# Feed-forward end of a hybrid decoder layer: the last two outputs made in two shares of tokens

## The chip, the cores and the metric

The kernel runs on one core of a Trainium2 chip. The metric is the device time of one execution in microseconds (us). Before the change three runs took 1458.08, 1457.53 and 1454.21 us; their median is 1457.53.

## The reference, cut to what matters

One decoder layer with two head groups, then a gated feed-forward network and a last RMS norm, on 320 tokens (256 of a prompt and 8 x 8 of samples) of width 2048. The part that the change touches is the end:

```python
h2 = rms_norm(x, norm_ffn)
gate, up = jnp.split(h2 @ w_ffn_in, 2, axis=-1)
x = x + (jax.nn.silu(gate) * up) @ w_ffn_out
...
y_prompt = rms_norm(xp, norm_final)
y_sample = rms_norm(xs, norm_final)
```

The hidden width is 5632. The norm of a token needs the squares of all its 2048 features, so no output can be normed before the last feature block of that token is there.

## The kernel before

Activations lie transposed: features on the 128 partitions, in `KT` = 16 blocks, and the `N` = 320 tokens along the free axis. `x1[:, n]` is block `n` of the residual, 128 x 320 in f32. Every large product is made by `gemm`: each f32 weight block is split into a rounded part `hi` (type fp32r) and a rest `lo`, the activations likewise, and three matmuls of 128x128 weights and 320 columns are added up in PSUM (lines 141 to 143). `wload` fetches the weights, up to eight 128x128 blocks at a time: SyncE issues the load (line 129), ScalarE rounds (`hi`, line 130), VectorE subtracts (`lo`, line 131). Its buffers come from a pool named by `wpool`; from the first feed-forward chunk on that is `wp2` with four raw and three split buffers, while the earlier pool `wp` also serves the sample states of the retention heads (`states_load`, `states_add`).

The hidden features are worked through in `FCH` = 4 chunks of 11 blocks. `ffn_in(c)` makes a chunk, `ffn_out(c, a)` multiplies it into the 16 outputs: for each output `n` 33 matmuls into `ps_fo`, which VectorE adds to `x1[:, n]` (lines 174 to 177, the helper `tt`; it stands in the trace as line 176). In the last chunk ScalarE also squares the finished block (`sqx`), VectorE sums the squares in `acc3`, and ScalarE multiplies the block with the norm's weight (line 1168).

The end of the program works so. `rstd_bcast` finds the norm's factor: matmuls of the squares with a column of ones give each token's sum (`ps_r`, and `ps_l` for the last block, whose square comes latest), with tokens as partitions, in three groups of 128 that begin at the tokens of `STARTS`; VectorE makes the reciprocal root in three Newton rounds (`rsqrt`, on `ms`, `ry`, `rt` of three columns); matmuls with the identity lay it out again along the tokens on all partitions (`ps_r2`, in the trace also `ps_r<-ident,ry`). In between `keep_warm` lets TensorE multiply ones. Then ScalarE copies the factor into `acc3`, VectorE scales blocks 0 to 10 from PSUM and GpSimd blocks 11 to 15 from that copy, and SyncE stores them in eight transfers, block groups by the table `TAIL`:

```python
    next(tail["rg"])
    rps = next(tail["rg"])
    act.copy(acc3, rps)
    for a_, b_ in TAIL:
        for n in range(a_, b_):
            tt(x1[:, n], x1[:, n], rps, MUL)
            if n < 5:
                pool.tensor_tensor(x1[:, 11 + n], x1[:, 11 + n], acc3, MUL)
        sp.dma_start(yT[:, a_:b_], x1[:, a_:b_])
    sp.dma_start(yT[:, 11:14], x1[:, 11:14])
    sp.dma_start(yT[:, 14:16], x1[:, 14:16])
```

TensorE and GpSimd work in the order in which the program is written; on the other engines a scheduler orders the instructions, and `tc.high_priority(offset=...)` moves those inside it ahead in that order. Every engine works through its queue in order.

Of the kernel before, what the change touches and what calls it, by code (L numbers as in the profile page):

```python
# [12 lines left out]
F32 = mybir.dt.float32  # L13
F32R = mybir.dt.float32r
I32 = mybir.dt.int32
AF = mybir.ActivationFunctionType
ALU = mybir.AluOpType
ADD, SUB, MUL = ALU.add, ALU.subtract, ALU.mult
PSUM = bass.MemoryType.PSUM

P = 128
D = 2048
KT = D // P
NP, NB, NS = 256, 8, 8
N = NP + NB * NS
# [3 lines left out]
FCH = 4  # L29
FCT = FT // FCH  # L30
# [5 lines left out]
TAIL = ((0, 1), (1, 2), (2, 3), (3, 5), (5, 8), (8, 11))  # L36
# [8 lines left out]
def hybrid_kernel(ctx, tc, xT, w_in, w_in4, w_out, w_glu, w_fi, w_fo, vecs, s5p, bc, x0,  # L45
# [3 lines left out]
    pe, act, dve, pool, sp = nc.tensor, nc.scalar, nc.vector, nc.gpsimd, nc.sync  # L49

    cst = ctx.enter_context(tc.tile_pool(name="cst", bufs=1))
    wp = ctx.enter_context(tc.tile_pool(name="wp", bufs=1))
    ps_acc = ctx.enter_context(tc.tile_pool(name="ps_acc", bufs=2, space=PSUM))

    def f(t):
        return t.bitcast(F32)
# [18 lines left out]
    def v(nm, i):  # L75
        return vec[:, voff[nm] + i:voff[nm] + i + 1]


    class Clk:
        now = 0.0  # L80
        n = 0
# [9 lines left out]
    def run_due(flush=False):  # L91
        while clk.heap and (flush or clk.heap[0][0] <= clk.now):
            t, _, gen = heapq.heappop(clk.heap)
            clk.now = max(clk.now, t)
            try:
                d = next(gen)
            except StopIteration:
                continue
            spawn(gen, d)

    def mm(cost, *a, **k):
        pe.matmul(*a, **k)
        clk.now += cost
# [8 lines left out]
    def keep_warm(n):  # L112

        pt = ps_acc.tile([P, 512], F32, name="warm_ps", tag="acc", bufs=2)
        for _ in range(n):
            pe.matmul(pt, onesr, onesr.unsqueeze(1).to_broadcast([P, 4, P]), start=True, stop=True)


    wpool = [wp, (3, 3, 3)]

    def wload(src, nk, offset=3000):

        out = []
        with tc.high_priority(offset=offset):
            for k0 in range(0, nk, 8):
                m = min(8, nk - k0)
                raw, hi, lo = (wpool[0].tile([P, 8, P], d, name=n, tag=n, bufs=wpool[1][i])
                               for i, (n, d) in enumerate((("raw", F32), ("hi", F32R), ("lo", F32R))))
                sp.dma_start(raw[:, :m], src[:, k0:k0 + m])
                act.copy(hi[:, :m], raw[:, :m])  # L130
                dve.tensor_tensor(lo[:, :m], raw[:, :m], f(hi[:, :m]), SUB)  # L131
                out += [(hi[:, i], lo[:, i]) for i in range(m)]
        return out

    def gemm(name, src, nk, xhi, xlo, ps=None, ws=None):
        ws = ws or wload(src, nk)
        if ps is None:
            pt = ps_acc.tile([P, 512], F32, name=name, tag="acc", bufs=2)
            ps = pt[:, :N]
        for k, (hi, lo) in enumerate(ws):  # L140
            pe.matmul(ps, hi, xhi[:, k], start=k == 0, stop=False)  # L141
            pe.matmul(ps, hi, xlo[:, k], start=False, stop=False)  # L142
            pe.matmul(ps, lo, xhi[:, k], start=False, stop=k == nk - 1)  # L143
            clk.now += 0.4
            if k < nk - 1:
                run_due()
        return ps
# [20 lines left out]
    def ts(out, a, s1, o1, s2=None, o2=None):  # L168
        if o2 is None:
            dve.tensor_scalar(out, a, s1, None, o1)  # L170
        else:
            dve.tensor_scalar(out, a, s1, s2, o1, o2)
        return out

    def tt(out, a, b, op):
        dve.tensor_tensor(out, a, b, op)  # L176
        return out

    def stt(out, a, s, b, o1, o2):
        dve.scalar_tensor_tensor(out, a, s, b, o1, o2)  # L180
        return out

    def rsqrt(t, y, tmp):

        ts(y.bitcast(I32), t.bitcast(I32), -0.5, MUL, float(0x1EF759DF), ADD)
        for _ in range(3):
            tt(tmp, y, y, MUL)
            tt(tmp, tmp, t, MUL)
            stt(y, tmp, 1.5, y, ADD, MUL)

    STARTS = (0, 128, 192)
# [1 line left out]
    EVAC = 1500  # L193
    GN = 1000

    def rstd_bcast(pool_, acc, ps_of, tag, last=None, dl=5.0, ytok=None):

        def sums(a, name):
            ps = ps_of(name)
            for i, s in enumerate(STARTS):  # L200
                mm(0.1, ps[:, i:i + 1], a[:, s:s + P], ones[:, 0:1], start=True, stop=True)
            return ps[:, 0:3]

        ms = pool_.tile([P, 3], F32, name="ms", tag=tag + "ms")
        y = pool_.tile([P, 3], F32, name="ry", tag=tag + "ry")
        if ytok is not None:
            ytok.append(y)
        tmp = pool_.tile([P, 3], F32, name="rt", tag=tag + "rt")
        ps = sums(acc, "ps_r")
        if last is not None:  # L210
            keep_warm(3)
        with tc.high_priority(offset=2000):
            ts(ms, ps, -0.5 / D, MUL, -0.5 * EPS, ADD)
            if last is not None:
                stt(ms, sums(last(), "ps_l"), -0.5 / D, ms, MUL, ADD)
            if last is not None:
                keep_warm(9)
            rsqrt(ms, y, tmp)
        yield dl
        ps2 = ps_of("ps_r2")  # L220
        for i, s in enumerate(STARTS):
            mm(0.22, ps2[:, s:s + P], y[:, i:i + 1].to_broadcast([P, P]), ident, start=True,
               stop=True)
        yield ps2[:, :N]
# [680 lines left out]
    with tc.issue_after(los[4].ins):  # L905
        s5_params(exps[0])
    ytok = []
    rg = rstd_bcast(s5, accq, misc, "n1", ytok=ytok)

    def finish_norm():  # L910
# [47 lines left out]
    x1 = xp.tile([P, KT, N], F32, name="x1")  # L958
# [69 lines left out]
    for n in range(KT):  # L1028
        if n == 0:
            late = gemm_late("ps_o", lambda n: w_out[n, :, 8:16], 0, 4, 8, rhi, rlo)  # L1030
        ps = late[n] if n < 2 else gemm("ps_o", w_out[n, :, 8:16], 8, rhi, rlo)
# [4 lines left out]
    for n in range(8):  # L1036
        ps = gemm("ps_g", w_glu[n], 8, yhi, ylo)
# [5 lines left out]
    hp = ctx.enter_context(tc.tile_pool(name="hp", bufs=1, reuse_waits="tile"))  # L1043
# [5 lines left out]
    def square(n, pl):  # L1049
        s = pl.tile([P, N], F32, name="sqx", tag="sqx", bufs=2)  # L1050
        act.activation(s, x1[:, n], AF.Square)
        return s

    for n in range(KT):
        if n == 0:
            late = gemm_late("ps_o2", lambda n: w_out[n, :, 0:8], 0, 6, 8, zhi, zlo)
        ps = late[n] if n < 2 else gemm("ps_o2", w_out[n, :, 0:8], 8, zhi, zlo)
# [5 lines left out]
        else:  # L1063
            s = square(n, hp)
# [7 lines left out]
    fp = ctx.enter_context(tc.tile_pool(name="fp", bufs=1, side="right", reuse_waits="tile"))  # L1072
# [5 lines left out]
    def ffn_norm():  # L1078
        rg = rstd_bcast(hp, acc2, norm_ps, "n2")
        next(rg)  # L1080
        yield DL["n2b"]
        act.copy(rbc2, next(rg))
# [65 lines left out]

    wp2 = ctx.enter_context(tc.tile_pool(name="wp2", bufs=1, reuse_waits="tile"))
    acc3 = fp.tile([P, N], F32, name="acc3")  # L1150
    tail = {}

    def ffn_out(c, a):
        for n in range(KT):
            ps = gemm("ps_fo", w_fo[c, n], FCT, *a)
            if c == FCH - 1 and n == KT - 1:
                tail["rg"] = rstd_bcast(fp, acc3, norm_ps, "n3", lambda: tail["s"])
            tt(x1[:, n], x1[:, n], ps, ADD)
            if c == FCH - 1:
                if n == 0:  # L1160
                    act.activation(acc3, x1[:, n], AF.Square)
                else:
                    s = square(n, hp)
                    if n == KT - 1:
                        tail["s"] = s
                    else:
                        tt(acc3, acc3, s, ADD)
                act.mul(x1[:, n], x1[:, n], v("g_fin", n))

    a0 = ffn_in(0)  # L1170
    a1 = ffn_in(1)
    ffn_out(0, a0)
    a2_ = ffn_in(2)
    ffn_out(1, a1)
    a3 = ffn_in(3)
    ffn_out(2, a2_)
    ffn_out(3, a3)
    next(tail["rg"])
    rps = next(tail["rg"])
    act.copy(acc3, rps)  # L1180
    for a_, b_ in TAIL:
        for n in range(a_, b_):
            tt(x1[:, n], x1[:, n], rps, MUL)
            if n < 5:
                pool.tensor_tensor(x1[:, 11 + n], x1[:, 11 + n], acc3, MUL)
        sp.dma_start(yT[:, a_:b_], x1[:, a_:b_])
    sp.dma_start(yT[:, 11:14], x1[:, 11:14])
    sp.dma_start(yT[:, 14:16], x1[:, 14:16])


def _host(inp):
# [92 lines left out]
```

## Time and profile before

| | us |
|---|---|
| median of three runs | 1457.53 |
| the profiled execution, its own time | 1454.4 |
| its span, first to last instruction | 1452.3 |
| TensorE busy in it | 1435.0 |
| VectorE busy | 852.8 |
| ScalarE busy | 607.5 |
| GpSimd busy | 80.7 |

PE is TensorE's matmuls and PEld its weight loads, DVE is VectorE, ACT ScalarE, POOL GpSimd, SP SyncE (SPq its queue, from which transfers are issued). A row gives a start or a sum in us, a length, and for a group the mean of one instruction in ns. Matmuls overlap: the length of one runs from its start to the end of its results, and a matmul can start long before the one ahead has ended, so the pace of a run is read from the distance of starts. An f32 matmul stands in the trace as two passes, each with its own weight load; an fp32r matmul as one. Times in the tables of stages and in the timelines count from the start of the span.

### The profile page before, as it was taken

How to read it: one execution, taken by the hardware profiler on the slowest of the kernel's cores; microseconds unless marked ns; L12 is line 12 of the kernel's file. 1: busy time of each engine (PE TensorE's matmuls, PEld its weight loads, DVE VectorE, ACT ScalarE, POOL GpSimd, SP SyncE). 2: the span in 40 equal slices, each digit the busy share in tenths (PEclk: the TensorE clock that was granted, in tenths of full speed). 3: DMA queues.
4: the chain of work that ended last, by engine and by line, in shares of the span. 5: the costliest groups of instructions: out<-in, count | busy, mean ns of one | idle time of the engine just before them, and what ended most of it. 6: DMA issues, size and time to landing. Idle time of an engine off the chain costs nothing.

```text
span 1452.3 us, 26302 instructions
## 1 busy us (share of the span) xinstructions
PE 1435.0 (99%) x10654; PEld 1419.5 (98%) x10654; DVE 852.8 (59%) x1402; ACT 607.5 (42%) x973; POOL 80.7 (6%) x163
## 2 busy tenths in 40 slices
PE   9999999999999999999999999999999999999997
PEld 8999999999999999999999999999999999999996
DVE  8978787777566747564444444444444444444454
ACT  7555555555355433333333333333333333333452
POOL 8520001100000000000000000000000000000001
PEclk9999999999999999999999999999999999999998
DMA  8455554555644575665444455444355444444443
GB/s 286 161 162 156 164 165 150 155 162 151 208 149 154 177 229 182 225 198 166 149 155 146 122 154 175 147 156 148 120 154 164 159 153 151 136 137 145 154 146 111
DMA packets 84712, 235.38 MB, mean 162 GB/s; under 512 B 16368, under 2 KB 32368, under 8 KB 84592
## 3 DMA queue, kind: packets, MB, share of 16 engines
q1 hardware_dynamic: 83680, 231.58, 49.8%
q10 hardware_dynamic: 912, 2.14, 0.5%
q8 instruction: 84, 1.38, 0.4%
q14 instruction: 36, 0.29, 0.1%
HBM read 222.63 MB, written 8.95 MB: 159 GB/s over the span
## 4 chain that ended last, share of the span: by engine, by line
PE 70%; DVE 1%; ACT 0%; issue 0%; DVEq 0%
PE ps_fo L142 7%; PE ps_fu L141 7%; PE ps_fo L141 7%; PE ps_fu L142 7%; PE ps_fu L143 7%; PE ps_fo L143 7%; PE ps_fg L141 7%; PE ps_fg L142 7%; PE ps_fg L143 7%; PE ps_o L141 1%; PE ps_o L142 1%; PE ps_o L143 1%; PE ps_g L142 1%; PE ps_g L143 1%; PE ps_g L141 1%; DVE x L176 0%
## 5 line engine op out<-in xcount | busy, mean ns | idle before, releaser
L131 DVE TENSOR_TENSOR lo<-raw,hi 128x1024 fp32r<-128x1024 f32 (+1 forms) x416 | 466.6, 1122 | 381.8 <-ACT hi L130 381.1
L130 ACT CAST hi<-raw 128x1024 fp32r<-128x1024 f32 (+1 forms) x416 | 402.1, 967 | 673.4 <-PE ps_fo L142 189.2
L141 PE MATMUL ps_fg<-hhi,hi 128*128 128x320 f32 x704 | 217.5, 309 | 0.0
L142 PE MATMUL ps_fo<-alo,hi 128*128 128x320 f32 x704 | 217.5, 309 | 0.0
L143 PE MATMUL ps_fo<-ahi,lo 128*128 128x320 f32 x704 | 217.5, 309 | 0.0
L141 PE MATMUL ps_fo<-ahi,hi 128*128 128x320 f32 x704 | 217.5, 309 | 0.0
L142 PE MATMUL ps_fg<-hlo,hi 128*128 128x320 f32 x704 | 217.4, 309 | 0.0
L142 PE MATMUL ps_fu<-hlo,hi 128*128 128x320 f32 x704 | 217.4, 309 | 0.0
L141 PE MATMUL ps_fu<-hhi,hi 128*128 128x320 f32 x704 | 217.4, 309 | 0.0
L143 PE MATMUL ps_fg<-hhi,lo 128*128 128x320 f32 x704 | 217.4, 309 | 0.0
L143 PE MATMUL ps_fu<-hhi,lo 128*128 128x320 f32 x704 | 217.4, 309 | 0.0
L141 PE MATMUL ps_p<-xhi,hi 128*128 128x320 f32 x560 | 177.7, 317 | 1.9 <-DVE q__1095 L176 1.4
L143 PE MATMUL ps_p<-xhi,lo 128*128 128x320 f32 x560 | 173.2, 309 | 0.0
L142 PE MATMUL ps_p<-xlo,hi 128*128 128x320 f32 x560 | 172.9, 309 | 0.0
L142 PEld LDWEIGHTS ps_fg<-hlo,hi 128*128 128x128 f32 x704 | 132.3, 188 | 0.3
L141 PEld LDWEIGHTS ps_fg<-hhi,hi 128*128 128x128 f32 x704 | 132.3, 188 | 0.3
L142 PEld LDWEIGHTS ps_fu<-hlo,hi 128*128 128x128 f32 x704 | 132.4, 188 | 0.0
L141 PEld LDWEIGHTS ps_fu<-hhi,hi 128*128 128x128 f32 x704 | 132.4, 188 | 0.0
L143 PEld LDWEIGHTS ps_fu<-hhi,lo 128*128 128x128 f32 x704 | 132.4, 188 | 0.0
L143 PEld LDWEIGHTS ps_fg<-hhi,lo 128*128 128x128 f32 x704 | 132.3, 188 | 0.0
L141 PEld LDWEIGHTS ps_fo<-ahi,hi 128*128 128x128 f32 x704 | 132.1, 188 | 0.0
L142 PEld LDWEIGHTS ps_fo<-alo,hi 128*128 128x128 f32 x704 | 132.1, 188 | 0.0
(420 smaller groups left out, 1939.4 us busy)
## 6 DMA issues: line engine op xcount, KB each, us to landing
raw<-w_fi SPq DMA_DIRECT2D x176, 512.0 KB, 3.7
raw<-w_in SPq DMA_DIRECT2D x79, 512.0 KB, 4.1
raw<-w_fo SPq DMA_DIRECT2D x64, 512.0 KB, 3.5
raw<-w_out SPq DMA_DIRECT2D x32, 512.0 KB, 3.7
raw<-w_fo SPq DMA_DIRECT2D x64, 192.0 KB, 2.4
rt<-r SPq DMA_DIRECT2D x8, 512.0 KB, 5.2
raw<-w_glu SPq DMA_DIRECT2D x8, 512.0 KB, 3.6
raw<-r SPq DMA_DIRECT2D x8, 512.0 KB, 4.3
```

What stands on the lines that cost most here:

```text
L130: act.copy(hi[:, :m], raw[:, :m])
L131: dve.tensor_tensor(lo[:, :m], raw[:, :m], f(hi[:, :m]), SUB)
L141: pe.matmul(ps, hi, xhi[:, k], start=k == 0, stop=False)
L142: pe.matmul(ps, hi, xlo[:, k], start=False, stop=False)
L143: pe.matmul(ps, lo, xhi[:, k], start=False, stop=k == nk - 1)
```

## The change

The last two outputs (`n` = 14 and 15) of the last chunk leave `ffn_out`'s loop and go to `out_tail`. It loads both weights, the second from the pool `wp`, and then goes over two shares of the tokens, 0 to 191 and 192 to 319: in each share it makes output 14 and then output 15, with matmuls of 192 and of 128 columns. The first share's squares are summed by `rstd_bcast` with two groups of tokens; its first step is written behind output 14 of the second share, its second step (the broadcast) behind output 15. `finish` scales and stores one share: it is what stood at the program's end, on a slice of the tokens. The second share has a factor of its own, one group of tokens, with the warming matmuls. `add_out` is what `ffn_out` did to an output in the last chunk.

```diff
@@ rstd_bcast @@
-    def rstd_bcast(pool_, acc, ps_of, tag, last=None, dl=5.0, ytok=None):
+    def rstd_bcast(pool_, acc, ps_of, tag, last=None, dl=5.0, ytok=None, starts=STARTS):
+        nst = len(starts)
...
-            for i, s in enumerate(STARTS):
+            for i, s in enumerate(starts):
...
@@ the end of the feed-forward part @@
+    ps_t = ctx.enter_context(tc.tile_pool(name="ps_t", bufs=2, space=PSUM))
...
     def ffn_out(c, a):
+        lastc = c == FCH - 1
+        for n in range(KT - 2 if lastc else KT):
             ps = gemm("ps_fo", w_fo[c, n], FCT, *a)
...
+        if lastc:
+            out_tail(c, a)
+
+    def finish(rps, sl):
+        acc = acc3[:, sl]
+        act.copy(acc, rps)
+        for a_, b_ in TAIL:
+            for n in range(a_, b_):
+                tt(x1[:, n, sl], x1[:, n, sl], rps, MUL)
+                if n < 5:
+                    pool.tensor_tensor(x1[:, 11 + n, sl], x1[:, 11 + n, sl], acc, MUL)
+            sp.dma_start(yT[:, a_:b_, sl], x1[:, a_:b_, sl])
+        sp.dma_start(yT[:, 11:14, sl], x1[:, 11:14, sl])
+        sp.dma_start(yT[:, 14:16, sl], x1[:, 14:16, sl])
+
+    TA = 192
+
+    def out_tail(c, a):
+        sls = (slice(0, TA), slice(TA, N))
+        ws = []
+        for n in (KT - 2, KT - 1):
+            ws.append(wload(w_fo[c, n], FCT))
+            wpool[:] = [wp, (3, 3, 3)]
+        rga = rstd_bcast(hp, acc3, norm_ps, "n2", starts=(0, TA - P))
+        sq = []
+        for j, sl in enumerate(sls):
+            for i, n in enumerate((KT - 2, KT - 1)):
+                pool_, tag = ((ps_acc, "acc"), (ps_t, "t"))[j]
+                pt = pool_.tile([P, 512], F32, name="ps_fo", tag=tag, bufs=2)
+                ps = gemm("ps_fo", None, FCT, a[0][:, :, sl], a[1][:, :, sl], ps=pt[:, :sl.stop - sl.start], ws=ws[i])
+                with tc.high_priority(offset=4000):
+                    add_out(n, ps, sl, sq if j and i else None)
+                if j and not i:
+                    next(rga)
+        rps = next(rga)
+        finish(rps[:, sls[0]], sls[0])
+        with tc.high_priority(offset=4000):
+            rgb = rstd_bcast(fp, acc3, norm_ps, "n3", lambda: sq[0], starts=(TA,))
+            next(rgb)
+            rps = next(rgb)
+        finish(rps[:, sls[1]], sls[1])
```

How the instructions stand at three places. First TensorE at the very end of the program; `ps_fo` are the products, `ps_r<-ones` and `ps_l` the sums of squares, `ps_r` with a number the broadcast of a factor. Before:

```order
L143 MATMUL ps_fo<-ahi,lo 128x320
L102 MATMUL ps_r<-ones,acc_6466 128x1 x3
L116 MATMUL warm_ps<-ones 128x512 x3
L102 MATMUL ps_l<-ones,sqx 128x1 x3
L116 MATMUL warm_ps<-ones 128x512 x9
L102 MATMUL ps_r_15444<-ident,ry 128x128 x3
```

And with the change, from the last three products of the second share on:

```order
L141 MATMUL ps_fo<-ahi,hi 128x128
L142 MATMUL ps_fo<-alo,hi 128x128
L143 MATMUL ps_fo<-ahi,lo 128x128
L102 MATMUL ps_r_15505<-ident,ry 128x128 x2
L102 MATMUL ps_r<-ones,acc_6466 128x1
L116 MATMUL warm_ps<-ones 128x512 x3
L102 MATMUL ps_l<-ones,sqx 128x1
L116 MATMUL warm_ps<-ones 128x512 x9
L102 MATMUL ps_r_15566<-ident,ry 128x128
```

The broadcast of the first share's factor (`ps_r_15505`) stands behind the last product of the second share; the second share's sums, warming and broadcast follow it.

Second, VectorE behind its last addition of a product; `ms`, `ry` and `rt` belong to the reciprocal root. Before:

```order
L176 TENSOR_TENSOR x_4939<-x_4939,ps_fo 128x320
L172 TENSOR_SCALAR ms<-ps_r 128x3
L180 SCALAR_TENSOR_TENSOR ms<-ps_l,ms 128x3
L172 TENSOR_SCALAR ry<-ms 128x3
L176 TENSOR_TENSOR rt<-ry 128x3
L176 TENSOR_TENSOR rt<-rt,ms 128x3
```

And with the change, where the last row stands for the second share's scaling and the pairs between go on in the same way up to it:

```order
L176 TENSOR_TENSOR x_4939<-x_4939,ps_fo 128x128
L172 TENSOR_SCALAR ms<-ps_r 128x1
L176 TENSOR_TENSOR x_4939<-x_4939,ps_r_15505 128x192
L180 SCALAR_TENSOR_TENSOR ms<-ps_l,ms 128x1
L176 TENSOR_TENSOR x_4939<-x_4939,ps_r_15505 128x192
L172 TENSOR_SCALAR ry<-ms 128x1
L176 TENSOR_TENSOR x_4939<-x_4939,ps_r_15505 128x192
L176 TENSOR_TENSOR rt<-ry 128x1
L176 TENSOR_TENSOR x_4939<-x_4939,ps_r_15505 128x192
...
L176 TENSOR_TENSOR x_4939<-x_4939,ps_r_15566 128x128 x11
```

The eleven scalings of the first share now alternate with the steps of the second share's reciprocal root, and the second share's scalings follow in one run.

Third, SyncE in the first feed-forward chunk, with the change (`rs_o` is a store of a sample state, `w_fi` and `w_fo` are weights of the two feed-forward products):

```order
L1121 DMA rs_o<-raw 128x1024 [waits DVE_49]
L129 DMA raw<-w_fi 128x1024 [waits DMAHW2_49,DVE_49]
L129 DMA raw<-w_fo 128x1024 [waits DMAHW7_49]
L129 DMA raw<-w_fi 128x1024 [waits DMAHW4_49,DVE_49]
L129 DMA raw<-w_fi 128x1024 [waits DMAHW5_49,DMAHW3_49,DVE_49]
L129 DMA raw<-w_fi 128x1024 [waits DMAHW6_49,DVE_49]
L1121 DMA rs_o<-raw 128x1024 [waits DVE_49]
L129 DMA raw<-w_fo 128x384 [waits DMAHW1_49,DVE_49,Activation_49]
L129 DMA raw<-w_fi 128x1024 [waits DMAHW0_49,DVE_49]
```

The two `w_fo` rows are the weights of output 15, which stood at the end of the weight loads before; here they wait for transfers (DMAHW), which the rows around them show as state stores.

## Rows read from the trace of the kernel before

**Rows 1.** The page, part 1: busy us (share of the span) and instructions.
```profile
PE 1435.0 (99%) x10654; PEld 1419.5 (98%) x10654; DVE 852.8 (59%) x1402; ACT 607.5 (42%) x973; POOL 80.7 (6%) x163
```

**Rows 2.** Stages: stretch, its length, engines' busy us, granted clock, DMA share, GB/s.
```profile
1426.80:1436.70 9.90, 9.90 (x71) 9.90 (x69) 3.65 (x6) 3.54 (x6) 0.00 (x0) 1.00 0.00 0
1436.70:1442.30 5.60, 5.00 (x29) 3.92 (x29) 2.44 (x13) 1.46 (x3) 0.00 (x0) 1.00 0.00 0
1442.30:1446.80 4.50, 0.00 (x0) 0.00 (x0) 4.46 (x11) 0.00 (x1) 4.15 (x5) 0.77 0.54 210
1446.80:1451.40 4.60, 0.00 (x0) 0.00 (x0) 0.00 (x1) 0.00 (x0) 0.00 (x0) 0.50 0.90 365
```

**Rows 3.** Timeline of PE from 1435 us: start, length, line, operation, count.
```profile
1436.23 0.31 PE L142 MATMUL ps_fo<-alo,hi 128*128 128x320 f32 x1
1436.38 0.31 PE L143 MATMUL ps_fo<-ahi,lo 128*128 128x320 f32 x1
1436.53 0.72 PE L102 MATMUL ps_r<-ones,acc 128*128 128x1 f32 x6
1437.89 0.72 PE L102 MATMUL ps_l<-ones,sqx 128*128 128x1 f32 x6
1438.48 2.31 PE L116 MATMUL warm_ps<-ones 128*128 128x512 f32 x9
1440.94 0.91 PE L102 MATMUL ps_r<-ident,ry 128*128 128x128 f32 x6
```

**Rows 4.** Timeline of DVE from 1436 us; in brackets idle time before, and its releaser.
```profile
1436.72 0.49 DVE L176 TENSOR_TENSOR x<-x,ps_fo 128x320 f32<-128x320 f32 x1 [3.32 <-PE ps_fo L143]
...
1438.66 0.16 DVE L180 SCALAR_TENSOR_TENSOR ms<-ps_l,ms 128x3 f32<-128x3 f32 x1 [1.21 <-PE ps_l L102]
1438.85 0.17 DVE L172 TENSOR_SCALAR ry<-ms 128x3 int32<-128x3 int32 x1
1439.06 0.16 DVE L176 TENSOR_TENSOR rt<-ry 128x3 f32<-128x3 f32 x1
...
1440.63 0.16 DVE L180 SCALAR_TENSOR_TENSOR ry<-rt,ry 128x3 f32<-128x3 f32 x1
1442.34 4.47 DVE L176 TENSOR_TENSOR x<-x,ps_r 128x320 f32<-128x320 f32 x11 [1.55 <-ACT acc L1180]
```

**Rows 5.** Timeline of ACT from 1436 us.
```profile
1437.25 0.47 ACT L1051 ACTIVATE sqx<-x 128x320 f32<-128x320 f32 x1 [3.77 <-DVE x L176]
...
1441.88 0.43 ACT L1180 COPY acc<-ps_r 128x320 f32<-128x320 f32 x1 [3.56 <-PE ps_r L102]
```

**Rows 6.** Timelines of POOL, then of SP, at the end.
```profile
1442.38 4.15 POOL L1185 TENSOR_TENSOR x<-x,acc 128x320 f32<-128x320 f32 x5 [1102.62 <-ACT acc L1180]
...
1446.83 0.34 SPq L1186 DMA_DIRECT2D yT<-x  x1
1447.29 1.02 SPq L1188 DMA_DIRECT2D yT<-x  x1
```

**Rows 7.** Stores by size (count, KB, median us to landing), then the last store's.
```profile
yT<-x SPq DMA_DIRECT2D x3, 480.0 KB, 3.6
yT<-x SPq DMA_DIRECT2D x3, 160.0 KB, 1.9
...
DMA to landing us min/median/max: 4.1/4.1/4.1
```

**Rows 8.** Timeline of PEld, the weight loads, at the end.
```profile
1436.23 0.19 PEld L143 LDWEIGHTS ps_fo<-ahi,lo 128*128 128x128 f32 x1
...
1437.77 0.76 PEld L102 LDWEIGHTS ps_l<-ones,sqx 128*128 128x128 f32 x6 [0.15 <-ACT sqx L1051]
...
1440.90 0.74 PEld L102 LDWEIGHTS ps_r<-ident,ry 128*128 128x128 f32 x6 [0.54 <-issue]
```

**Rows 9.** Waits of SP's queue from 560 to 700 us: total, times, longest.
```profile
SPq L1103 <- DMA rs_o<-raw: 7.2, 5, 2.9
```

**Rows 10.** A stage of these waits, columns as in the second group.
```profile
600.00:620.00 20.00, 20.00 (x137) 19.83 (x136) 12.05 (x16) 7.14 (x8) 0.00 (x0) 1.00 0.62 215
```

**Rows 11.** Groups of PE from 50 to 56 us by shape: busy us, mean ns.
```profile
L102 PE MATMUL pss<-q__768,k__776 128*128 128x256 f32 x2 | 0.6, 380 | 0.0
...
L102 PE MATMUL pss<-q__768,k__776 128*128 128x128 f32 x2 | 0.4, 274 | 0.0
```

More of the change, by code (lines that the diff above doesn't have):

```diff
@@ L194, in hybrid_kernel @@
     GN = 1000
-    def rstd_bcast(pool_, acc, ps_of, tag, last=None, dl=5.0, ytok=None):
+    def rstd_bcast(pool_, acc, ps_of, tag, last=None, dl=5.0, ytok=None, starts=STARTS):
+        nst = len(starts)
         def sums(a, name):
             ps = ps_of(name)
-            for i, s in enumerate(STARTS):
+            for i, s in enumerate(starts):
                 mm(0.1, ps[:, i:i + 1], a[:, s:s + P], ones[:, 0:1], start=True, stop=True)
-            return ps[:, 0:3]
-        ms = pool_.tile([P, 3], F32, name="ms", tag=tag + "ms")
-        y = pool_.tile([P, 3], F32, name="ry", tag=tag + "ry")
+            return ps[:, 0:nst]
+        ms = pool_.tile([P, nst], F32, name="ms", tag=tag + "ms")
+        y = pool_.tile([P, nst], F32, name="ry", tag=tag + "ry")
         if ytok is not None:
             ytok.append(y)
-        tmp = pool_.tile([P, 3], F32, name="rt", tag=tag + "rt")
+        tmp = pool_.tile([P, nst], F32, name="rt", tag=tag + "rt")
         ps = sums(acc, "ps_r")
@@ L220, in rstd_bcast @@
         ps2 = ps_of("ps_r2")
-        for i, s in enumerate(STARTS):
+        for i, s in enumerate(starts):
             mm(0.22, ps2[:, s:s + P], y[:, i:i + 1].to_broadcast([P, P]), ident, start=True,
@@ L1150, in hybrid_kernel, with add_out @@
     acc3 = fp.tile([P, N], F32, name="acc3")
+    ps_t = ctx.enter_context(tc.tile_pool(name="ps_t", bufs=2, space=PSUM))
     tail = {}
+    def add_out(n, ps, sl, last=None):
+        tt(x1[:, n, sl], x1[:, n, sl], ps, ADD)
+        if n == 0:
+            act.activation(acc3[:, sl], x1[:, n, sl], AF.Square)
+        else:
+            sq = hp.tile([P, N], F32, name="sqx", tag="sqx", bufs=2)
+            s = sq[:, sl]
+            act.activation(s, x1[:, n, sl], AF.Square)
+            if last is None:
+                tt(acc3[:, sl], acc3[:, sl], s, ADD)
+            else:
+                last.append(sq)
+        act.mul(x1[:, n, sl], x1[:, n, sl], v("g_fin", n))
@@ L1153, in ffn_out @@
     def ffn_out(c, a):
-        for n in range(KT):
+        lastc = c == FCH - 1
+        for n in range(KT - 2 if lastc else KT):
             ps = gemm("ps_fo", w_fo[c, n], FCT, *a)
[L1156 to L1168, printed above, removed]
+            if lastc:
+                add_out(n, ps, slice(0, N))
+            else:
+                tt(x1[:, n], x1[:, n], ps, ADD)
@@ new lines, in ffn_out @@
+        if lastc:
+            out_tail(c, a)
[10 more added lines that the diff above has]
+        sp.dma_start(yT[:, 14:16, sl], x1[:, 14:16, sl])
@@ L1177, in hybrid_kernel @@
     ffn_out(3, a3)
[L1178 to L1188, printed above, removed]
 def _host(inp):
```

## The prediction

> **What bounds the kernel now.** I read the engine totals first: TensorE is busy 1435.0 us of a span of 1452.3 us [rows 1]. So only its idle stretches and what follows its last product can be shortened, and the change touches the second. The stage table says how that end is made up [rows 2]: up to 1436.7 us TensorE is full and the DMA engines move nothing; for 5.6 us a norm factor is found with little work anywhere; for 4.5 us VectorE and GpSimd scale; then 4.6 us in which only DMA works, at a share of 0.90. The timelines give the chain. The last product starts at 1436.38 and takes 0.31 us [rows 3], so it ends at 1436.69. VectorE adds it at 1436.72, the factor is ready at 1440.79, scaling starts at 1442.34 and ends at 1446.81 [rows 4]. The last store is issued at 1447.29 [rows 6] and lands 4.1 us later [rows 7], at 1451.4; another 0.9 us passes until the span ends. From the last product to the end: 15.6 us.
>
> **What the change really moves.** The words are that the first share is stored while the second is made. The order on TensorE says otherwise: the two matmuls that broadcast the first share's factor stand behind all 66 products of the second share. TensorE works in order, so no token can be scaled before the last product ends. What does move under the second share's products is only the first share's sum and its rsqrt. The second share still needs sum, rsqrt, broadcast, scaling and stores afterwards.
>
> **Step 1, the products.** Removed: 66 matmuls of 320 columns at 0.147 us from start to start (1436.23 to 1436.38 [rows 3]), 9.7 us. Added: 66 of 192 and 66 of 128 columns. Each loads 128x128 weights, so the weights are loaded twice as often. No product of this rounded type in the trace has fewer than 320 columns. From below the price follows the columns: 0.088 and 0.059 us, 9.7 us together. From above it is that of plain f32 (rival 1), 35.8 us. The nearest rows are runs of f32 passes that each load 128x128 weights: six loads take 0.74 or 0.76 us [rows 8], less the length of one (0.19), over five: 0.110 to 0.114. It is the same with 128 moving columns (the first) and with one (the second), so there the load sets the pace and not the columns. The products' own loads last 0.19 us each, like these [rows 8]. I take 0.112 for both widths: 132 x 0.112 = 14.8 us. The first share's sum, two f32 matmuls or four passes, now stands among them: 0.45 us. It waits for nothing: its operand is complete some 1.5 us after the first share's last product (0.49 us on VectorE, 0.47 on ScalarE, as much again on VectorE, at 320 columns [rows 4, 5]), while the 33 products ahead of it take 3.7 us. Step 1: 14.8 + 0.45 - 9.7 = **+5.55 us**; the last product ends at 1442.2.
>
> **Step 2, to the first share's scaling.** Before, 5.65 us from the last product to the first scaling. Now the factor is ready, and there remain four broadcast passes and the copy. Six passes take 0.91 us [rows 3], four 0.91 - 2 x 0.112 = 0.69; the ScalarE copy takes 0.43 at 320 columns [rows 5], some 0.3 here. Scaling starts about 1443.25: 0.9 us later than before, not earlier.
>
> **Step 3, the second share's factor.** TensorE must finish the broadcast, then one sum, three warm passes and the last sum. Before, the last product's end to the use of the last sum took 1436.69 to 1438.66, 1.97 us; four passes are added ahead, and two sums of three matmuls shrink to one each (eight passes less), net four less, 0.45 us; square and add shorten too, but the warm passes cover that. I take 1.6: 1443.8. The rsqrt was 2.13 us (1438.66 to 1440.79), ten dependent steps at 0.197 us. Now ten scalings of the first share stand between these steps on VectorE. A step of 3 columns is 0.16 us long, a scaling of 320 is 0.48 long and 0.40 apart from the next ((4.47 - 0.48) / 10) [rows 4]; between these, 1.0 ns a column: 192 columns 0.35 long and 0.27 apart, 128 columns 0.29 and 0.21. A pair costs between 0.27 + 0.08 and 0.27 + 0.197. I take 0.35, since a step's wait for its predecessor passes under the scaling between: 3.65 us in all, ready at 1447.45.
>
> **Step 4, to the end.** From factor to broadcast 0.15 us, two passes 0.46, copy 0.3, hand-overs 0.06 (at a granted clock of 0.50, which TensorE has some time after its work ends [rows 2], the passes would take about 0.2 more, not counted): scaling of the second share starts at 1448.42. Eleven scalings at 0.21: first done 1448.71, last 1450.8 (before 1446.81). GpSimd does its five at 0.83 each of 320 columns [rows 6], two fifths to all of that here, 1.7 to 4.2 us; I take 1.8, so it ends by 1450.4. SyncE's queue now holds 16 stores. The first share's eight (pieces of 768 B) are issued while the second's factor is made. The second's eight need about 0.45 us each (0.34 to issue, 1446.83 to the next at 1447.29 [rows 6]): the last is issued at 1448.75 + 7 x 0.45 = 1451.9. Its landing costs from 1.9 us (median of the 160 KB stores) to 4.1 us, that of the present last one, which stands behind a full queue [rows 7]; I take 1.9, because only 1.05 MB are left and they arrive at the pace of the issues. With the 0.9 us at the end: 1454.7. **Sum: 1454.7 - 1452.3 = +2.4 us.**
>
> **Costed at nothing.** The weights of output 15 now come from another pool, and their two loads move far forward, into the first feed-forward chunk, on SyncE, ScalarE and VectorE. On SyncE each stands a row or so behind a state store whose buffer it reuses, so the queue waits there for that store to land, with weight loads behind it. The same wait exists five times there now, longest 2.9 us, 7.2 in all [rows 9], and in the stage of these waits TensorE is busy 20.00 of 20.00 us [rows 10]. The cover is the four weight buffers; if it were gone, each wait would cost up to 2.9 us.
>
> **Rivals.**
> 1. *Narrow products run like plain f32* (the slower side). Two widths of one f32 product, 256 and 128 columns, take 380 and 274 ns a pass [rows 11]: 0.83 ns a column, and each such matmul stands as two passes. The 320-column products show 0.46 ns a column in one pass. If the fast pace holds only for wide operands, 192 columns cost 2 x 0.159 and 128 cost 2 x 0.112 (the load's pace): 66 x 0.542 = 35.8 us, 21.0 more than my sum, **1481**. In its half form (one pass at 0.83 ns) 66 x (0.159 + 0.112) = 17.9 us, 3.1 more, **1463.0**. For it: no narrow one is in the trace. Against: loads of equal length in both types [rows 8], and one matmul for each product in the order. It makes the kernel measurably slower once the mean of the 132 products passes 0.127 us (2.0 us more than my sum). Chances 0.13 and 0.08.
> 2. *The reload hides.* Then the products still take 9.7 us, step 1 is +0.45 and the sum 2.4 - 5.1 = -2.7: **1454.8**. Against: the f32 runs above. Chance 0.07. The Trainium skill, TensorE: Matmul & The Clock Gate, section Back-to-back issue gap, gives about 81 ns for a pair of load and matmul at 128 columns; by that the products would take some 11.2 us by our estimate and the kernel 1456.3. The f32 runs show 110 to 114 ns [rows 8], which disagrees, and I go by the rows.
> 3. *The store queue ends late.* The second share's stores have two or three short pieces a partition. If the five of them each hold SyncE for 1.02 us, as the last store does now [rows 6], and the last lands in 3.6 us [rows 7], 3.0 + 1.7 = 4.7 us are added: **1464.6**. Against: 1.02 us is seen only behind a full queue. Chance 0.10.
>
> **How the numbers follow.** The profiled execution took 1454.4 us for its span of 1452.3; the median of the three runs is 1457.53, 3.1 above it. I add the sum to the median: 1457.5 + 2.4 = **1459.9 us**, chance 0.62, with 1458 to 1463 as its own range (pairs at 0.47 add 1.2 us, a landing of 3.6 us 1.7; issues at 0.34 take off 0.8). A measurement of this kernel can tell about 0.3%, 4.4 us, from no change. Slower by more: rival 1 with 0.13 and 0.07, rival 3 with 0.06, the forecast's own tail 0.05, together 0.31. Faster by more needs over 4.4 us gained, beyond rival 2: 0.03. The rest, 0.66, is within. The range 1454.3 to 1466 leaves out the full form of rival 1 and some tails.
>
> **What would show it.** In the profile after: 192- and 128-column products some 0.112 us apart (0.088 and 0.059 is rival 2; 0.16 or 0.32 is rival 1); the last product ending near 1442.2; first scaling of the first share about 1 us after it; VectorE's pairs 0.35 us apart; no store of outputs before the last product; stores of the second share issued 0.45 us apart, and no new idle time of TensorE between 560 and 700 us. I am wrong in kind if any output is stored while TensorE still multiplies, or if the last product ends after 1444.

## The result and the profile after

The changed kernel takes 1460.63 us (median of 20 executions, 1457.74 to 1462.59); the kernel before, timed beside it, 1455.57 us (20 executions, 1454.06 to 1458.08). The ratio is 1.0031, with a 95% interval of 1.0024 to 1.0037: **4.5 us slower** (3.5 to 5.4); the two medians by themselves are 5.1 us apart. Timed a second time, in the last section of experiments below, the ratio was 1.0041 (1.0027 to 1.0055). I had predicted 1459.9 us and +2.4. The direction and the absolute time are right, the size of the change is not: it is 2 to 3 us too small. That the absolute time fits so well is partly luck, since the three runs of the kernel before that I added the sum to had a median of 1457.53, 2 us above that of the twenty.

The profiled executions differ by more than that, 1459.9 against 1452.3 us of span, and 3.3 us of it lie at the start of the program: the first product of the last two outputs starts at 1430.17 us in the one and 1426.85 in the other. This is not the change's doing. The difference is there already at the first product of the feed-forward part (505.19 and 501.86 us), ahead of the loads that the change moves, the first of which is issued at 643.9 us; from that product to the first of the last two outputs both kernels take 924.98 us, to 0.01. In the kernel that only splits the stores (below), whose program up to there is that of before, that product starts at 1430.55, and among the thirteen profiles at full clock its start lies between 1426.85 and 1432.50. One more profiled execution, of the kernel with the early broadcast, took 2359.42 us at a mean granted clock of 0.556 and is left out of every number here. So I compare **tails**: from the start of the first product of outputs 14 and 15 to the end of the span. Before 25.45 us, after 29.73 in the first profile and 29.21 in a second one: +4.3 and +3.8. The two differ by 0.5 us, and most of the other kernels have one profile, so a difference of some tenths between tails tells nothing.

The page's engine totals of the kernel after, which answer to [rows 1]:

```profile
span 1459.9 us, 26473 instructions
PE 1441.8 (99%) x10716; PEld 1427.1 (98%) x10716; DVE 858.2 (59%) x1428; ACT 607.7 (42%) x978; POOL 80.3 (5%) x168
```

Its stages at the end, with the columns of [rows 2]: products; broadcast of the first share; first share's scaling with the second share's rsqrt; second broadcast; second scaling; stores.

```profile
1430.00:1445.46 15.46, 15.46 (x140) 15.46 (x139) 4.59 (x20) 3.38 (x8) 0.00 (x0) 1.00 0.00 1
1445.46:1446.40 0.94, 0.94 (x9) 0.90 (x8) 0.47 (x3) 0.57 (x3) 0.00 (x0) 1.00 0.00 0
1446.40:1451.30 4.90, 2.75 (x14) 1.96 (x12) 4.57 (x22) 0.24 (x1) 2.84 (x5) 0.99 0.28 89
1451.30:1452.50 1.20, 0.80 (x2) 0.50 (x2) 0.04 (x1) 0.27 (x1) 0.00 (x0) 0.50 1.09 369
1452.50:1454.80 2.30, 0.00 (x0) 0.00 (x0) 2.22 (x11) 0.00 (x0) 2.11 (x5) 0.50 1.10 364
1454.80:1459.90 5.10, 0.00 (x0) 0.00 (x0) 0.00 (x0) 0.00 (x0) 0.00 (x0) 0.50 0.61 182
```

In the first row, 15.46 us long, TensorE never pauses, and the DMA engines move 1 GB/s: no output leaves while the products run. That is the heart of the matter, and it was visible in the order of the instructions before any run. TensorE's timeline, which answers to [rows 3]:

```profile
1437.30 0.27 PE L142 MATMUL ps_fo<-alo,hi 128*128 128x192 f32 x1
1437.41 0.27 PE L143 MATMUL ps_fo<-ahi,lo 128*128 128x192 f32 x1
...
1438.05 0.27 PE L143 MATMUL ps_fo<-ahi,lo 128*128 128x128 f32 x1
1438.16 0.28 PE L141 MATMUL ps_fo<-ahi,hi 128*128 128x128 f32 x1
...
1445.19 0.27 PE L143 MATMUL ps_fo<-ahi,lo 128*128 128x128 f32 x1
1445.31 0.66 PE L102 MATMUL ps_r<-ident,ry 128*128 128x128 f32 x4
```

192 and 128 columns stand equally far apart, 0.11 us. The first share's broadcast follows the last product at once. VectorE's timeline, which answers to [rows 4]:

```profile
1446.38 0.35 DVE L176 TENSOR_TENSOR x<-x,ps_r 128x192 f32<-128x192 f32 x1
1447.04 0.16 DVE L180 SCALAR_TENSOR_TENSOR ms<-ps_l,ms 128x1 f32<-128x1 f32 x1 [0.30 <-PE ps_l L102]
1447.11 0.34 DVE L176 TENSOR_TENSOR x<-x,ps_r 128x192 f32<-128x192 f32 x1
1447.37 0.14 DVE L172 TENSOR_SCALAR ry<-ms 128x1 int32<-128x1 int32 x1
1447.44 0.34 DVE L176 TENSOR_TENSOR x<-x,ps_r 128x192 f32<-128x192 f32 x1
1447.70 0.46 DVE L176 TENSOR_TENSOR rt<-ry 128x1 f32<-128x1 f32 x1
1448.08 0.34 DVE L176 TENSOR_TENSOR x<-x,ps_r 128x192 f32<-128x192 f32 x1
1448.34 0.37 DVE L176 TENSOR_TENSOR rt<-rt,ms 128x1 f32<-128x1 f32 x1
...
1448.90 0.37 DVE L180 SCALAR_TENSOR_TENSOR ry<-rt,ry 128x1 f32<-128x1 f32 x1
...
1449.46 0.14 DVE L176 TENSOR_TENSOR rt<-ry 128x1 f32<-128x1 f32 x1
...
1451.13 0.15 DVE L180 SCALAR_TENSOR_TENSOR ry<-rt,ry 128x1 f32<-128x1 f32 x1
1452.46 2.26 DVE L176 TENSOR_TENSOR x<-x,ps_r 128x128 f32<-128x128 f32 x11 [1.19 <-ACT acc L1185]
```

The small steps of the second share's rsqrt stand between the first share's scalings; most last 0.14 to 0.16 us, three of them 0.46, 0.37 and 0.37. SyncE's stores, which answer to [rows 6]; the second share's begin with the second row:

```profile
1446.76 3.15 SPq L1191 DMA_DIRECT2D yT<-x  x3
...
1452.78 3.31 SPq L1191 DMA_DIRECT2D yT<-x  x6
1456.18 0.50 SPq L1192 DMA_DIRECT2D yT<-x  x1
1456.77 0.49 SPq L1193 DMA_DIRECT2D yT<-x  x1
```

### The profile page after: what moved, and what is told of

Same layout as the page of the kernel before. It is cut to its first block, busy times and chain, and to the rows that moved or that the text cites. A ratio compares the mean times of both kernels' runs of the same rounds, so it can differ in the third digit from the quotient of the medians.

```text
span 1459.9 us, 26473 instructions
## 1 busy us (share of the span) xinstructions
PE 1441.8 (99%) x10716; PEld 1427.1 (98%) x10716; DVE 858.2 (59%) x1428; ACT 607.7 (42%) x978; POOL 80.3 (5%) x168
## 4 chain that ended last, share of the span: by engine, by line
PE 70%; DVE 0%; issue 0%; ACT 0%; DVEq 0%
PE ps_fo L143 7%; PE ps_fo L142 7%; PE ps_fo L141 7%; PE ps_fu L142 7%; PE ps_fg L142 7%; PE ps_fg L141 7%; PE ps_fu L143 7%; PE ps_fg L143 7%; PE ps_fu L141 7%; PE ps_o L143 1%; PE ps_o L141 1%; PE ps_o L142 1%; PE ps_g L142 1%; PE ps_g L143 1%; PE ps_g L141 1%; DVE x L176 0%
## 5 line engine op out<-in xcount | busy, mean ns | idle before, releaser
L143 PE MATMUL ps_fo<-ahi,lo 128*128 128x320 f32 (+2 forms) x726 | 222.8, 307 | 0.0
L142 PE MATMUL ps_fo<-alo,hi 128*128 128x320 f32 (+2 forms) x726 | 222.8, 307 | 0.0
L141 PE MATMUL ps_fo<-ahi,hi 128*128 128x320 f32 (+2 forms) x726 | 222.8, 307 | 0.0
L141 PEld LDWEIGHTS ps_fo<-ahi,hi 128*128 128x128 f32 x726 | 136.5, 188 | 0.0
L143 PEld LDWEIGHTS ps_fo<-ahi,lo 128*128 128x128 f32 x726 | 136.4, 188 | 0.0
L142 PEld LDWEIGHTS ps_fo<-alo,hi 128*128 128x128 f32 x726 | 136.4, 188 | 0.0
```

## Experiments

My theory after the result: a product cannot be cheaper than its weight load, so the split costs 5 us of TensorE; sixteen stores and narrower scalings cost another 1.5; and the overlap, which could pay for this, returns little, because the first share's broadcast stands behind the second share's products. The main rival: the products cost little, and the later stages (rsqrt between scalings, the store queue) make the kernel slower.

### The products alone

```
-                    add_out(n, ps, sl, sq if j and i else None)
-                if j and not i:
-                    next(rga)
...
+        rg = rstd_bcast(fp, acc3, norm_ps, "n3", lambda: sq)
+        next(rg)
+        rps = next(rg)
+        finish(rps, slice(0, N))
```

> Only the products of the last two outputs are made in two shares (192, then 128 columns); one norm factor, one scaling and eight stores as in the kernel before. Theory (each product costs its weight load, 0.111 us whatever its width): 132 x 0.1113 - 66 x 0.1466 = 14.69 - 9.68 = +5.0 us against the kernel before, the rest of the end unchanged, so 15.5 to 16 us from the last product to the end of the span and a ratio of about 1.0034. Rival (the products cost little, and the later stages make the kernel slower): from first to last product of the two outputs under 11 us, ratio within 0.001 of 1.

Measured: ratio 1.0040 (1.0027 to 1.0054), tail 30.82 us, +5.4. From the start of the first to that of the last product 14.57 us, before 9.53: +5.04, as expected. What comes behind it takes as long as before up to the last store's issue (10.90 and 10.91 us from the start of the last product); from there to the end it takes 5.35 us, before 5.01, and this 0.3 us has no explanation here. TensorE's rows, of either width:

```profile
1434.80 0.27 PE L142 MATMUL ps_fo<-alo,hi 128*128 128x192 f32 x1
1434.91 0.27 PE L143 MATMUL ps_fo<-ahi,lo 128*128 128x192 f32 x1
...
1435.22 0.28 PE L143 MATMUL ps_fo<-ahi,lo 128*128 128x128 f32 x1
1435.33 0.27 PE L141 MATMUL ps_fo<-ahi,hi 128*128 128x128 f32 x1
```

By the tails the split of the products alone costs more than the whole change does (+5.4 against +4.3 and +3.8); the ratios, whose intervals overlap, do not tell the two apart. The products are not cheap, so the rival is out.

### Two other widths, 256 and 64

```
-    TA = 192
+    TA = 256
```

> As the run with only the products in two shares, but shares of 256 and 64 columns. Theory (a product costs the longer of its weight load, 0.111 us, and its columns at the pace of the 320-column products, 0.1466 / 320 = 0.458 ns each): 256 columns 0.117 us apart, 64 columns 0.111 us apart, 66 x 0.117 + 66 x 0.111 = 15.1 us for the two outputs. Rival (the narrow products cost a fixed amount more than their columns): 64 columns closer together than 0.10 us, 256 further apart than 0.125 us.

Measured: the 66 products of 256 columns take 7.77 us (1429.73 to 1437.50), 0.118 us each, and the 64-column ones are 0.111 apart: the longer of load and columns, as the theory says. That the floor belongs to the load, and not to any matmul whatever its weights, I did not test by a run, but the kernel before has a row on it: 16 plain f32 passes with weights of 32 columns, 0.28 us long each, stand (0.64 - 0.28) / 15 = 0.024 us apart.

```profile
61.48 0.64 PE L102 MATMUL po<-rt,qg 128*32 128x128 f32 x16
```

Yet the tail was 35.67 us. At 1443.34, with TensorE busy without a pause, the 64-column products were suddenly 0.213 us apart. The granted clock, by stretches before and after that moment, with the columns of [rows 2]:

```profile
1438.20:1443.30 5.10, 5.10 (x48) 5.10 (x47) 0.44 (x2) 1.49 (x4) 0.00 (x0) 1.00 0.00 0
1443.30:1446.10 2.80, 2.80 (x16) 2.80 (x15) 0.00 (x0) 0.00 (x0) 0.00 (x0) 0.52 0.03 6
```

I had not expected this, so I ran the kernel again.

> The kernel with the products in shares of 256 and 64 columns once more, to see whether the fall of the granted clock in the 64-column products is the kernel's own. If it is: the clock falls from 1.00 to 0.50 some 5 to 6 us into the 64-column products again, and the products from there are 0.21 us apart. If it was a disturbance of that one execution: 0.111 us apart to the last product, and no fall before it.

The clock fell again, 2.8 us into the 64-column products (1441.00; they start at 1438.18) where it was 5.8 us the first time, to 0.50; the tail was 38.89 us. So it is the kernel's own, but not its moment. The sum of 15.1 us that I had expected for the products holds only while the clock stays at 2.4 GHz: from the start of the first to that of the last they took 16.1 and 18.9.

### The stores alone

```
+        for sl in (slice(0, TA), slice(TA, N)):
+            finish(rps[:, sl], sl)
```

> The products of the last two outputs stay whole (320 columns) and one norm factor is found; only the scaling and the stores are made in two shares of tokens, with 16 stores. Theory (16 issues on SyncE's queue and 22 narrower scalings set the end): VectorE's scalings take 11 x 0.27 + 11 x 0.21 = 5.3 us in place of 4.47, the second share's eight issues follow its scaling at 0.45 to 0.6 us each, so +1 to +2 us against the kernel before. Rival (the number of issues costs nothing, the amount of data sets the end): within 0.5 us of the kernel before. A second rival (the smaller pieces halve the rate of the stores): +4 us.

Measured: ratio 1.0008 (1.0000 to 1.0017), tail 26.95 us, +1.5: the theory. VectorE's two scalings take 3.00 and 2.27 us where one took 4.47 [rows 4], and the last issue follows the start of the second by 5.1 us. VectorE, then SyncE's last issue:

```profile
1445.93 3.00 DVE L176 TENSOR_TENSOR x<-x,ps_r 128x192 f32<-128x192 f32 x11 [1.44 <-ACT acc L1185]
1449.26 2.27 DVE L176 TENSOR_TENSOR x<-x,ps_r 128x128 f32<-128x128 f32 x11 [0.33 <-ACT acc L1185]
...
1454.39 0.49 SPq L1193 DMA_DIRECT2D yT<-x  x1
```

With the products alone this gives the **bill**: 5.4 + 1.5 = 6.9 us of cost in the tails, of which the change shows 4.3 and 3.8. By the tails its overlap returns 2.6 to 3.1 us. The ratios give less: 5.8 and 1.2 us for the parts, 4.5 and 6.0 for the change, so 1.0 to 2.5, with intervals of 1 to 2 us on either side of each.

### The first share's broadcast ahead of the last products

```
-                if j and not i:
-                    next(rga)
-        rps = next(rga)
-        finish(rps[:, sls[0]], sls[0])
+        early = {(1, 0): {4: first_sum}, (1, 1): {1: first_out}}
...
+            if k in at:
+                at[k]()
```

> The kernel after, but the first share's sum stands 5 weight blocks into the second share's output 14 and its broadcast 2 blocks into output 15, so TensorE reaches them about 3 us before its last product. Theory (the broadcast's place in TensorE's order is what keeps the first share from being scaled and stored under the products): the first stores are issued before the last product ends, the second share's rsqrt runs without scalings between its steps, about 1.6 us in place of 4.2, and the kernel is about 2.6 us faster than the kernel after, still 1.5 to 2 us slower than before, since the products keep their +5.0 us. Rival (the end is set by the number of stores on one queue, not by when they can start): the last store is issued at the same distance from the last product as in the kernel after, and the time moves by under 0.5 us.

Measured: 1.0008 (0.9999 to 1.0017), against 1.0031 and 1.0041 for the kernel after: about 3.3 us and 4.8 us less; the intervals do not touch. For the stages, one more profile of the same kernel:

> The same kernel as the one with the first share's sum and broadcast moved forward, for one profile at full clock. Theory: the first share's stores are issued before the last product ends; from the start of the last product to the end of the span 11.5 to 12.5 us, where the kernel after takes 14.7. Rival (the number of stores on one queue sets the end): 14 us or more from last product to end.

Tail 27.40 us, 1.8 to 2.3 less than in the two profiles after, near the 2.6 expected; 11.93 us from the start of the last product to the end. (This execution took 1461.83 us, because its first product of the last two outputs starts latest of all, at 1432.50.) Of TensorE (the last product), VectorE and SyncE:

```profile
1447.97 0.27 PE L143 MATMUL ps_fo<-ahi,lo 128*128 128x128 f32 x1
...
1445.67 3.00 DVE L178 TENSOR_TENSOR x<-x,ps_r 128x192 f32<-128x192 f32 x11 [0.56 <-ACT acc L1187]
1449.68 0.16 DVE L182 SCALAR_TENSOR_TENSOR ms<-ps_l,ms 128x1 f32<-128x1 f32 x1 [0.75 <-PE ps_l L102]
...
1452.65 2.26 DVE L178 TENSOR_TENSOR x<-x,ps_r 128x128 f32<-128x128 f32 x11 [0.88 <-ACT acc L1187]
...
1446.05 1.77 SPq L1193 DMA_DIRECT2D yT<-x  x4
```

The first share's scaling begins 2.3 us, and its first store is issued 1.9 us, before the last product starts. From there to the second share's scaling it takes 4.7 us instead of 7.3 and 7.0. The rsqrt in it took 2.1 us in place of 4.2; I had expected 1.6. This is what the change's words describe; the kernel after does not do it. It is still 2.0 us behind the kernel before by the tails: the bill of 6.9 less 4.9.

### GpSimd's part in the long steps

The three long steps end at 1448.16, 1448.71 and 1449.27. GpSimd's third to fifth scaling of the first share, in the kernel after, end at 1448.14, 1448.70 and 1449.26:

```profile
1447.54 0.60 POOL L1190 TENSOR_TENSOR x<-x,acc 128x192 f32<-128x192 f32 x1
...
1448.10 0.60 POOL L1190 TENSOR_TENSOR x<-x,acc 128x192 f32<-128x192 f32 x1
...
1448.66 0.60 POOL L1190 TENSOR_TENSOR x<-x,acc 128x192 f32<-128x192 f32 x1
```

So I left these five scalings out:

```
-                if n < 5:
+                if n < 5 and sl.start:
```

> The kernel after without GpSimd's five scalings of the first share (outputs 11 to 15 of the first 192 tokens stay unscaled); VectorE's work is the same. Theory (three of the small steps between the first share's scalings are 0.46, 0.37 and 0.37 us long because both their operands are in SBUF while GpSimd works on SBUF: they end within 0.03 us of the ends of GpSimd's third, fourth and fifth operation): all small steps take 0.14 to 0.16 us, all pairs 0.335 us apart, from the first small step to the last 3.5 to 3.6 us in place of 4.24, and the second share's scaling starts 0.6 to 0.7 us earlier after the last product (6.5 to 6.7 us in place of 7.27). Rival (SyncE's long second store issue, at the same time, holds VectorE up): the same three steps stay long.

VectorE's rows of the same three steps:

```profile
1448.56 0.15 DVE L176 TENSOR_TENSOR rt<-ry 128x1 f32<-128x1 f32 x1
...
1448.90 0.15 DVE L176 TENSOR_TENSOR rt<-rt,ms 128x1 f32<-128x1 f32 x1
...
1449.23 0.15 DVE L180 SCALAR_TENSOR_TENSOR ry<-rt,ry 128x1 f32<-128x1 f32 x1
```

All steps are short, first to last 3.48 us in place of 4.24. SyncE's long second issue (1.95 us in the first profile after) is not the cause: the long steps are there again in the second profile after, where it is missing, and here an issue of 1.29 us, from 1448.35, lies over the short ones. The second share's scaling starts 6.2 us after the start of the last product, even earlier than the 6.5 to 6.7 expected, because I had reckoned from the first profile after. In that one the granted clock had fallen to 0.50 when TensorE made the second broadcast (0.80 us long); here it stood at 1.00 (0.49 us), as in the second profile after, whose scaling starts 6.96 us after the last product: like for like, 0.8 us.

### Two store queues, and four stores

```
+        st = (sp, sp) if sl.start == 0 else (sp, act)
...
+            st[(a_, b_) in TAIL[1::2]].dma_start(yT[:, a_:b_, sl], x1[:, a_:b_, sl])
```

> The kernel after, but the second share's stores are issued by turns on SyncE and ScalarE. Theory (the last eight issues, at 0.5 us or more each on one queue, end later than the scaling that feeds them): the last issue comes 1.5 to 2 us after the second share's scaling starts plus its own length, in place of 4.3 us, and the kernel is 1.2 to 1.9 us faster than the kernel after. Rival (the DMA engines are what ends last, and the issues only wait their turn): the last landing is as late as in the kernel after, within 0.5 us.

Measured: 1.0023 (1.0013 to 1.0032), tail 29.03 us, only 0.2 to 0.7 below the kernel after. The ratio lies 1.2 and 2.6 us below the two of the kernel after, but its interval overlaps theirs, so the times leave open whether the 1.2 to 1.9 us that I had expected are there. The stretch from the second scaling's start to the end of the last issue, and from there to the end of the span, in the second profile of the kernel after:

```profile
1451.87:1456.48 4.61, 0.00 (x0) 0.00 (x0) 2.26 (x11) 0.00 (x0) 2.10 (x5) 0.73 0.84 263
1456.48:1459.10 2.62, 0.00 (x0) 0.00 (x0) 0.00 (x0) 0.00 (x0) 0.00 (x0) 0.50 0.43 127
```

and with two queues:

```profile
1450.95:1454.62 3.67, 0.00 (x0) 0.00 (x0) 2.26 (x11) 0.00 (x0) 2.11 (x5) 0.74 0.92 287
1454.62:1458.00 3.38, 0.00 (x0) 0.00 (x0) 0.00 (x0) 0.00 (x0) 0.00 (x0) 0.50 0.50 148
```

The issues end 0.9 us earlier and what follows them is 0.8 us longer. The first part of my theory holds, and by the profiles the gain does not follow: the rival, that the transfers end last, is nearer. The last stretch in which the DMA engines are full shows it, first with one queue, then with two:

```profile
1455.35:1457.45 2.10, 0.00 (x0) 0.00 (x0) 0.00 (x0) 0.00 (x0) 0.00 (x0) 0.50 1.12 338
```

```profile
1453.45:1456.00 2.55, 0.00 (x0) 0.00 (x0) 0.00 (x0) 0.00 (x0) 0.00 (x0) 0.50 1.10 324
```

It ends 5.6 us after the second scaling's start with one queue and 5.05 with two, and from there it is 1.65 and 2.0 us, nearly without data, to the end of the span. Both edits together:

> The kernel after with both: the first share's sum and broadcast early among the second share's products, and the second share's stores by turns on SyncE and ScalarE. Theory (the two gains are in different stretches, the first before the second share's scaling and the other behind it): about 1 us faster than the run with the early broadcast alone, so within 1 us of the kernel before, ratio 0.9995 to 1.0007. Rival (with the first share's stores out of the way, SyncE alone keeps up, or the DMA engines end last): the same time as with the early broadcast alone, ratio about 1.0008 or above.

Measured: 1.0015 (1.0007 to 1.0024), tail 27.25, against 1.0008 and 27.40 with the early broadcast alone. The rival again.

Fewer and larger stores, the other way to take issues off the queue:

```
+        for a_, b_ in (((0, 3), (3, 7), (7, 11)) if sl.start else TAIL):
...
+        for a_, b_ in (((11, 16),) if sl.start else ((11, 14), (14, 16))):
```

> The kernel after, but the second share leaves in four stores instead of eight (three of outputs 0 to 10, one of 11 to 15). Theory (eight issues on SyncE at 0.55 us each end later than the scaling): the last issue is over about 1 us earlier, 3.6 to 3.9 us after the start of the second share's scaling in place of 4.8, and the span ends 6.4 to 6.8 us after that start in place of 7.44. Rival (the data's own time on the DMA engines sets the end): the span still ends 7.2 to 7.6 us after it.

This run answers another question. The span ended 8.46 us after the start of the second scaling, later than either theory. The scheduler had put the store of outputs 11 to 15 first, and SyncE's queue stood behind it until GpSimd was done; the first share's data ran out at about 1451.7, and from there to 1453.2 no data moved. From SyncE's waits, then the stretch after GpSimd's end:

```profile
SPq L1193 <- POOL x L1190: 2.1, 1, 2.1
```

```profile
1452.50:1453.20 0.70, 0.00 (x0) 0.00 (x0) 0.01 (x1) 0.00 (x0) 0.00 (x0) 0.50 0.00 0
```

What four stores in the right order would give stays open.

### 224 and 96 columns, and the kernel after again

```
-    TA = 192
+    TA = 224
...
+            rgb = rstd_bcast(fp, acc3, norm_ps, "n3", lambda: sq[0], starts=(TA,), w=N - TA)
```

> As the run with the early broadcast, but shares of 224 and 96 columns. Theory (both widths still cost their weight load, 0.111 us each, and behind the last product only the second share's scaling and data count): the products take as long, the second share's scaling takes 11 x 0.17 = 1.9 us in place of 2.26, its data are 0.79 MB in place of 1.05, so 0.5 to 0.8 us less after the last product and a ratio to the kernel before of 1.0000 to 1.0006. Rival (96 columns are so narrow that the granted clock falls during the second share's products, as it did with 64): products 0.21 us apart in the last microseconds, and 2 us or more slower than with 192 and 128.

Measured: 1.0031 (1.0014 to 1.0048), against the 1.0000 to 1.0006 expected and 1.0008 (0.9999 to 1.0017) with 192 and 128; the two intervals just overlap. Five of its eight executions took 1458.2 to 1460.0 us at a mean granted clock of 0.996 to 0.998, three 1462.4 to 1466.3 at 0.991 to 0.992. The profiled one is of the five: products 0.111 us apart, tail 27.46, no gain over 27.40. The second scaling took 1.90 us, as expected, but from its start to the end of the span it was 7.13 us, against 7.25 with 128 columns and a third more data. The smaller amount of data also moved more slowly: in their full stretches the DMA engines moved 272 to 279 GB/s here, in pieces of 384 B, and 335 to 343 there, in pieces of 512 B. The three others have no trace; they fit the rival, but that is argued, not shown.

> The kernel after, a second time, beside the run with 224 and 96 columns. The time: ratio to the kernel before 1.0024 to 1.0037, as in its first comparison. Its profile: three of the small steps of the second share's rsqrt again end with GpSimd's third to fifth operation, and from the first product of the last two outputs to the end of the span 29.4 to 30.0 us, whatever the start of the program takes.

Measured: 1.0041 (1.0027 to 1.0055), a little over the expected band; tail 29.21, a little under. The long steps are there again, 0.46, 0.37 and 0.38 us.

No run beat the kernel before; the early broadcast came nearest, and its interval, 0.9999 to 1.0017, does not tell the two apart.

## Why the prediction was right, and where not

- **What bounds it, and the order on TensorE: right.** No output is stored before the last product ends; the first issue is at 1446.76, 1.3 us behind it. The last product ends at 1445.46, and I had named an end after 1444 as a sign of being wrong in kind. Counted from the first of these products it is not one: 3.32 us of it lie ahead of the change, and without them it ends at 1442.14, where I had 1442.2. I should have counted that sign from there.
- **Step 1: right.** From the first product to VectorE's add of the last 15.34 us (1430.17 to 1445.51), before 9.87: +5.47, predicted +5.55. The load's pace, read off f32 passes with one and with 128 columns [rows 8], holds for the rounded products at 64, 128 and 192 columns. Rivals 1 and 2 both fall with this. By the Trainium skill, TensorE: Matmul & The Clock Gate, section Back-to-back issue gap, the pair of load and matmul would be about 81 ns at 128 columns; the trace has 111.
- **Step 2: right.** The first share's scaling starts 0.9 us after the last product's end (1445.46 to 1446.38), predicted 1.05.
- **Step 3: start right, length wrong.** The last sum is used 1.58 us after the last product, predicted 1.6. Then the rsqrt took 4.24 and 4.25 us, predicted 3.65. Its pair of 0.35 us was good (0.333 for the undisturbed ones). The step that failed is "a step's wait for its predecessor passes under the scaling between", which counted only VectorE: three steps waited for GpSimd, and without it the sequence took 3.48. It cost **0.6 us**. The Trainium skill states this in SBUF — State Buffer, section Who interferes with whom: an instruction of VectorE with two SBUF inputs contends with one of GpSimd that reads SBUF. The trace agrees: the steps that waited have both inputs in SBUF, and the scalings between them, with one input in PSUM, did not wait.
- **Step 4: too short at both ends.** The hand-over from factor to scaling was 1.18 and 0.87 us, predicted 0.97; the higher one has the slow broadcast that I named and did not count. The last issue came 4.31 and 4.12 us after the scaling's start, predicted 3.48: they stood 0.54 to 0.57 us apart and not 0.45, a figure I had taken from one pair of issues in [rows 6]. From the last issue to the end it was 3.1 us, predicted 1.9 + 0.9. These two add **1.0 to 1.2 us**. The runs with two queues show that they do not add up freely: with the issues 0.9 us shorter, 0.8 us came back behind them. So the term that I mis-sized is the whole drain from the second scaling to the end, 7.2 to 7.4 us where I had 6.3. What sets this drain is only in part shown. Rival 3, with 4.7 us more (its own terms add up to 4.6), was far too dear.
- **Costed at nothing: right.** TensorE is busy 20.00 of 20.00 us between 600 and 620 us, as before [rows 10], and the whole feed-forward part up to the last two outputs takes 924.98 us, as before. SyncE's wait for the state stores is 7.6 us in five, longest 3.0 [rows 9], and one new wait of 1.0 us stands beside it.
- **The sum.** +2.4, less 0.1 in step 1, plus 0.6 in step 3, plus 0.95 and 1.16 for the drain, with 0.1 less and 0.2 more for the hand-over: 3.8 and 4.3, as the tails show. The measured ratio, 1.0031, lies at the edge of what I called no change. With the missing 2 us in the sum I should have given no change and slower about equal chances, not 0.66 and 0.31.

## What to carry to other kernels

A tile of moving columns can be split for free only while the columns, and not the weight load, set the pace: here 0.1466 us for 320 columns became twice 0.111. Before believing that one share's ending overlaps another's products, look for where its next matmul stands in TensorE's order; moving that one broadcast forward was worth more than every edit of queues and sizes (3.3 to 4.8 us by the ratios, 1.8 to 2.3 by the tails). And small dependent steps on VectorE are not free between its other work when GpSimd is reading SBUF.

## What was not expected of the hardware

The granted clock can fall from 2.4 to 1.2 GHz while TensorE is busy without a pause: in both executions with 64-column products it did, 5.8 and 2.8 us into them, after 66 products of 256 columns at full clock. With 128 columns it never did before the last product, in any of the eight profiles at full clock that have them. And SyncE's issues of the second share's stores, in pieces of 512 B, stood 0.54 to 0.57 us apart on average, against 0.46 for the last two in pieces of 1280 B before [rows 6].
